# Branch rows, residual rows and output weights get buffers of their own, and key transpositions are queued ahead of the softmax

## The chip, the cores and the metric

One core of one Trainium2 chip runs the whole program. The metric is the device time of one execution in microseconds (us), as the median of several runs. Less is better.

## What is computed

One step of a decoder layer in fp32 for two groups of tokens with the same weights: a prompt of 512 tokens (with 16 learned meta tokens ahead of it) and 8 sample requests of 8 tokens each, which attend to 2048 cached tokens in pages. In the kernel both groups are 576 columns (512 prompt, 64 sample).

```python
h = rmsnorm(x)                                  # 1024 wide
q, k, v, log_f, ..., gate_f, gate_g = split(h @ w_in)
o_fox = softmax(q k^T * scale + forget bias) v  # prompt: causal; sample: 2048 cached + 8 new tokens
o_gla = gated linear attention(...)             # chunked, with a state
merged = sigmoid(gate_f) * (o_fox @ w_fox_out) + sigmoid(gate_g) * (o_gla @ w_gla_out)
x = x + merged @ w_o
x = x + hier_moe(rmsnorm(x))                    # 32 experts: y += gate_e * ((silu(h w_g) * (h w_u)) w_d)
y = rmsnorm(x)
```

## The kernel before

**Numbers in two halves.** A large product is computed as three: each fp32 operand is split by `split` (L119) into a rounded high half (ScalarE, L123) and a low half, the difference (VectorE or GpSimd, L125), and `mm3` (L133) multiplies high by high, high by low and low by high. So every tile of weights (`wh`, `wl` from `w`) and every input (`ofh`, `ofl`, `ogh`, `ogl`) needs one ScalarE and one VectorE or GpSimd instruction ahead of TensorE.

**Stages.** First come norm, projections and the prompt's attention. From about 215 us on, the sample requests are worked off in small steps (`sample_steps`, L1009) between steps of other work: linear attention at first, and all along `dense`, a stream of projections of 24 matmuls a step that fills TensorE. In this stage TensorE's order is the program's order; a scheduler orders the other engines from dependencies and priorities, and each engine then works its own queue strictly in order. At about 563 us the stream ends; `merge` (L1066), the output projection `out_proj` (L1114) with the routing, and the experts (`moe`) follow.

**A sample request.** Keys and values arrive as gathered pages of 128x2048, four key pages (K) and four value pages (V) a request, issued on GpSimd's queue (POOL, L892) into rings of three buffers each. A key page is transposed in place on VectorE (`turn`, L1016), one ahead of its use; then 32 small matmuls make scores (S, L925). Behind the fourth page stands the softmax (L938 to L961, VectorE and ScalarE in turns), then transpositions of its result on TensorE (`tp<-ident,SP`, L967), then the products with V (L987). The step of the fourth page in `sample_s` runs up to the end of the softmax, and only then does the loop call `turn` for the next request's page. `QB` (L901) is the copy of a request's queries on POOL.

**The merge.** The prompt's branch results lie in DRAM (`ofd`, `ogd`); the last request's 64 columns lie in SBUF (`ofS`), and L1610 writes them to `ofd` when the last request is done. `merge` then loads both branches whole (`oraw`, L1073), splits them, loads two gate rows (`gt`, L1084) and loops over 8 column blocks of the output with two branches each: load a weight, split it, 48 matmuls, gate it on VectorE (`mt`).

**The output projection.** For 4 blocks of 256 columns a pair of weight tiles (`woh`, `wol`) is made in a ring `wo` of 2; the residual `x2` is loaded (L1127, L1128) behind the first pair's weights on SyncE's queue (SP), and every group of 24 matmuls is added onto it (L1139).

**The experts** read three weights of 1 MiB each: gate and up in one tile `wgu` (ring of 4 `wxg` + 1 `wxh`), down in `wdn` (2 `wxd` + 3 `wxe`). The first tiles of each ring are loaded ahead, from the start of the merge; afterwards each pair of experts asks for the tiles of a later pair, which wait for a free buffer.

## Time and profile before

| what | us |
|---|---|
| median of 3 runs | 1028.68 (1026.78 to 1032.39) |
| the profiled execution: its own time | 1023.5 |
| its span (first to last instruction) | 1021.8 |
| its mean granted TensorE clock | 0.949 |
| TensorE (PE) busy | 904.5 (89%) |
| VectorE (DVE) / ScalarE (ACT) / GpSimd (POOL) busy | 496.8 / 288.4 / 227.4 |

TensorE is busy nearly all the time, so a change matters where it idles or runs at a lower clock. Times below are us from the start of the span; a clock of 1.00 is 2.4 GHz, 0.50 is 1.2 GHz. In a timeline row a bracket at the end is the idle time ahead of the instruction and what ended it.

### The profile page before, as it was taken

To read this page: it belongs to the slowest core of one execution; us is meant where nothing else is said; L and a number is where in the kernel's file an instruction comes from. 1 tells how busy PE (TensorE), PEld (TensorE's weight loads), DVE (VectorE), ACT (ScalarE), POOL (GpSimd) and SP (SyncE) were. 2 spreads that over 40 slices of the span, in tenths; PEclk is the share of its full clock that TensorE was granted. 3 is DMA by queue.
4 is the path that set the end of the run, shared out by engine and by line. 5 is a ranking of instruction groups with operands and counts; after the bars stand their busy time and mean duration, and the time that the engine had idled before them with its cause. 6 is when DMAs were issued, how large, how long until landed. Compare 5 with 4: busy or idle time off the path is not lost.

```text
span 1021.8 us, 18903 instructions
## 1 busy us (share of the span) xinstructions
PE 904.5 (89%) x7768; PEld 695.1 (68%) x7768; DVE 496.8 (49%) x1123; ACT 288.4 (28%) x640; POOL 227.4 (22%) x354
## 2 busy tenths in 40 slices
PE   3989989986989899897899598699699999999994
PEld 3878868775879799886898598699434443444342
DVE  5643454549565558564651367115424432443345
ACT  4223445323142223322321233005321121112113
POOL 5320101324254323342210145012400000000001
PEclk9999979988899899998999799799799999999998
DMA  7243222196378778789989757811789999999712
GB/s 202 72 121 96 77 58 60 50 345 203 117 240 294 259 253 266 236 303 333 339 283 331 262 175 194 280 62 63 256 358 404 417 389 377 379 415 384 315 42 94
DMA packets 124319, 240.23 MB, mean 235 GB/s; under 512 B 15516, under 2 KB 89132, under 8 KB 107844
## 3 DMA queue, kind: packets, MB, share of 16 engines
q1 hardware_dynamic: 107700, 161.05, 45.2%
q0 software_dynamic: 11664, 72.36, 19.4%
q10 hardware_dynamic: 4864, 5.57, 1.6%
q8 instruction: 62, 1.02, 0.4%
q14 instruction: 29, 0.24, 0.1%
HBM read 226.66 MB, written 15.96 MB: 237 GB/s over the span
## 4 chain that ended last, share of the span: by engine, by line
PE 72%; DVE 9%; DMA 7%; ACT 4%; issue 3%; POOL 3%; another core or an unknown queue 0%; SPq 0%; POOLq 0%; DVEq 0%; ACTq 0%
PE pj L138 26%; PE pj L1330 11%; PE ab L1330 7%; PE dn L1330 5%; PE pj L1136 5%; PE S L925 3%; PE tp L987 2%; DVE K L1016 2%; PE tp L1333 2%; DMA V<-in_cache_v_dram,idx 1%; DMA x<-in_x_prompt_dram 1%; PE G L523 1%; DMA w<-in_w_o_dram 1%; PE tp L736 1%; DMA oraw<-ofd 1%
## 5 line engine op out<-in xcount | busy, mean ns | idle before, releaser
L138 PE MATMUL pj<-hth,wh 128*128 128x288 f32 (+2 forms) x656 | 207.5, 316 | 1.8 <-DVE kt L381 1.8
L138 PE MATMUL pj<-htl,wh 128*128 128x288 f32 (+2 forms) x656 | 200.2, 305 | 0.0
L138 PE MATMUL pj<-hth,wl 128*128 128x288 f32 (+2 forms) x656 | 199.8, 305 | 0.0
L138 PEld LDWEIGHTS pj<-hth,wh 128*128 128x128 f32 (+1 forms) x656 | 127.1, 194 | 11.7 <-issue 7.3
L138 PEld LDWEIGHTS pj<-htl,wh 128*128 128x128 f32 (+1 forms) x656 | 127.1, 194 | 1.2 <-issue 0.8
L138 PEld LDWEIGHTS pj<-hth,wl 128*128 128x128 f32 (+1 forms) x656 | 126.4, 193 | 1.1
L1330 PE MATMUL pj<-wgu,xt 128*64 128x512 f32 x512 | 118.6, 604 | 0.6
L1330 PEld LDWEIGHTS pj<-wgu,xt 128*64 128x64 f32 x512 | 38.1, 138 | 61.4 <-issue 56.6
L125 DVE TENSOR_TENSOR wl<-w,wh 128x1024 fp32r<-128x1024 f32 (+1 forms) x41 | 51.7, 1261 | 52.9 <-ACT wh L123 48.7
L1016 DVE STREAM_TRANSPOSE K<-K 128x2048 f32<-128x2048 f32 x32 | 73.6, 2301 | 0.4 <-DMA K<-in_cache_k_dram,idx 0.3
L123 ACT ACTIVATE wh<-w 128x1024 fp32r<-128x1024 f32 (+2 forms) x57 | 52.6, 925 | 60.4 <-PE pj L138 54.8
L1330 PE MATMUL ab<-yh,S 128*128 128x512 f32 (+1 forms) x160 | 66.6, 416 | 1.0 <-DVE x L1402 0.9
L1330 PE MATMUL ab<-yl,S 128*128 128x512 f32 (+1 forms) x160 | 62.9, 393 | 0.0
L1402 DVE TENSOR_TENSOR x<-x,ab 128x512 f32<-128x512 f32 (+1 forms) x80 | 54.5, 684 | 17.3 <-PE ab L1330 17.3
L925 PE MATMUL S<-K,QB 128*32 128x128 f32 x1024 | 38.8, 298 | 27.2 <-DVE K L1016 23.5
L1362 DVE SCALAR_TENSOR_TENSOR th<-th,pj 128x256 f32<-128x256 f32 x16 | 6.7, 421 | 112.1 <-ACT th L1361 112.1
L1330 PE MATMUL dn<-wdn,heT 128*64 128x512 f32 x256 | 57.7, 593 | 0.7 <-ACT heT L1371 0.7
L1303 POOL DMA_INDIRECT xg<-h2d,ix x16 | 16.1, 1005 | 182.4 <-PE tp L1333 180.4
L925 PEld LDWEIGHTS S<-K,QB 128*32 128x32 f32 x1024 | 29.6, 119 | 31.3 <-issue 24.8
L892 POOL DMA_INDIRECT V<-in_cache_v_dram,idx x32 | 31.5, 986 | 62.1 <-PE tp L987 42.3
L1330 PEld LDWEIGHTS dn<-wdn,heT 128*64 128x64 f32 x256 | 18.4, 137 | 36.8 <-issue 35.9
L1330 PEld LDWEIGHTS ab<-yh,S 128*128 128x128 f32 (+1 forms) x160 | 28.3, 177 | 21.5 <-DVE x L1402 14.6
(426 smaller groups left out, 1605.3 us busy)
## 6 DMA issues: line engine op xcount, KB each, us to landing
wgu<-in_w_expert_gate_dram SPq DMA_DIRECT2D x32, 1024.0 KB
wgu<-in_w_expert_up_dram SPq DMA_DIRECT2D x32, 1024.0 KB
wdn<-in_w_expert_down_dram SPq DMA_DIRECT2D x32, 1024.0 KB
w<-in_w_in_dram SPq DMA_DIRECT2D x40, 512.0 KB
gtd<-sm ACTq DMA_DIRECT2D x32, 144.0 KB
gt<-gtd SPq DMA_DIRECT2D x8, 576.0 KB
R<-rdr SPq DMA_DIRECT2D x16, 256.0 KB
w<-in_w_o_dram SPq DMA_DIRECT2D x8, 512.0 KB
```

Of the source, the lines that this page charges most:

```text
L123: keep(nc.scalar.activation(hi, raw, AF.Copy))
L125: keep(e.tensor_tensor(lo, raw, hi.bitcast(F32), op=OP.subtract))
L138: nc.tensor.matmul(ps, lhsT=w[:, kt, :], rhs=r[:, kt, cs], start=(kt == 0 and j == 0), stop=(kt == nk - 1 and j == 2))
L892: nc.gpsimd.indirect_dma_start(t, None, view, bass.IndirectOffsetOnAxis(ap=self.idx[:, which, i:i + 1], axis=0)))
L925: nc.tensor.matmul(S[32 * h4:32 * h4 + 32, hf, x * 128:(x + 1) * 128], lhsT=QB[:, hb].rearrange("p a b -> p (a b)"), rhs=Kv[:, hb], start= ...
L987: nc.tensor.matmul(po[32 * c:32 * c + 32, 0:128], lhsT=PTv[:, c // 2, x, g, :], rhs=vt[:, o + c * 128:o + c * 128 + 128], start=(n == 0), ...
L1016: self.tc.keep_in_program_order(nc.vector.transpose(t, t))
L1136: nc.tensor.matmul(ps[:w, 0:256], lhsT=M[s][:, a, kt, ts], rhs=b[:, kt, :], start=(kt == 0 and j == 0), stop=(kt == 7 and j == 2))
L1303: self.nc.gpsimd.indirect_dma_start(xg, None, self.h2d[:, :], bass.IndirectOffsetOnAxis(ap=col, axis=0), bounds_check=NQ - 1, oob_is_err=F ...
L1330: self.tc.keep_in_program_order(self.nc.tensor.matmul(*a, **kw))
L1333: self.tc.keep_in_program_order(self.nc.tensor.transpose(*a))
L1402: self.tc.keep_in_program_order(nc.vector.tensor_tensor(x, x, ps[:w], op=OP.add))
```

## The change

1. `turn()` is called in `sample_s` right behind each page's matmuls, so for the fourth page ahead of the softmax code instead of behind it.
2. New `branch_inputs`: once the linear attention has released its buffers, the branches' rows are loaded in 4 + 4 pieces (only the prompt's 512 columns of the first branch) and split on ScalarE and GpSimd, while the last requests run. The last request's 64 columns are split straight from `ofS`; the way through DRAM is gone. One step of `dense` is taken ahead of the last loop.
3. The first two gate rows are loaded before the stream ends (`gate_rows`).
4. `x2` has a buffer of its own and is loaded before `merge`.
5. The output weights lie in tiles of the experts' shape in a ring `wxo`, which later serves the experts: `wgu` ring of 6 (4 + 2), `wdn` ring of 4 (2 + 2). The early `wgu` loads now wait for buffers that come free after `merge`.

```diff
-    def sample_s(self, r, sw, keys):
+    def sample_s(self, r, sw, keys, turn):
...
                                          rhs=Kv[:, hb], start=(b == 0), stop=(b == 1))
+            turn()
         nc.gpsimd.memset(PN, 0.0)
...
                 if what == "s":
                     n += 1
-                    turn()
                 yield
...
+    def branch_inputs(self, op):
+
+        nc, hl = self.nc, []
+        with self.pool("obr", 1) as rp:
+            for nm, src, n in (("f", self.ofd, 512), ("g", self.ogd, NQ)):
+                raw = rp.tile([128, 4, n], F32, name=f"raw{nm}")
                 h = op.tile([128, 4, NQ], F32R, name=f"o{nm}h")
                 l = op.tile([128, 4, NQ], F32R, name=f"o{nm}l")
-                self.split(raw, h, l)
+                for m in range(4):
+                    nc.sync.dma_start(raw[:, m], src[m, :, 0:n])
+                    self.split(raw[:, m], h[:, m, 0:n], l[:, m, 0:n], "pool")
                 hl.append((h, l))
+        return hl
...
-            if not n:
-                nc.sync.dma_start(self.x2[:, 0:4, :], A["x_prompt"][0].rearrange("(i p) d -> p i d", p=128))
-                nc.sync.dma_start(self.x2[0:64, 4, :], A["x_sample"].rearrange("r t d -> (r t) d"))
...
+        up(5, **late)
...
-            for e in (5, 6):
+            for e in (6, 7):
                 up(2 * ep + e, pin=True)
-            for e in (3, 4) if ep else ():
+            for e in (2, 3) if ep else ():
                 dn(2 * ep + e, pin=True)
...
+                op = self.open("ohl", 1)
+                hl = self.branch_inputs(op)
+
+                step(dense)
                 while step(S):
                     step(S)
                     step(dense)
-                nc.sync.dma_start(self.ofd[:, :, 512:576].rearrange("m p t -> p m t"), self.ofS)
+                for x, y in zip(hl[0], (nc.scalar, nc.vector)):
+                    x = x[:, :, 512:576]
+                    if y is nc.scalar:
+                        y.activation(x, self.ofS, AF.Copy)
+                    else:
+                        y.tensor_tensor(x, self.ofS, hl[0][0][:, :, 512:576].bitcast(F32), op=OP.subtract)
+                mt = self.open("mtm", 2)
+                gs = [self.gate_rows(mt, m) for m in range(2)]
...
+            wo = self.ring("wxo", 2, side="right")
+            self.x2 = xp.tile([128, 5, D], F32, name="x2")
+            nc.sync.dma_start(self.x2[:, 0:4, :], A["x_prompt"][0].rearrange("(i p) d -> p i d", p=128))
+            nc.sync.dma_start(self.x2[0:64, 4, :], A["x_sample"].rearrange("r t d -> (r t) d"))
+            M = self.merge(mt, hl, gs)
...
-                self.moe(mp, gp, [Ring(wxg.pools + wxh.pools), Ring(wxd.pools + wxe.pools)])
+                self.moe(mp, gp, [Ring(wxg.pools + wo.pools), Ring(wxd.pools + wxe.pools)])
```

VectorE's queue at the softmax of the first request, before: the end of this softmax, with the key transposition behind it (L958, L961 are the softmax's last instructions, `sc`, `ge`, `rsT`, `sx` belong to the linear attention).

```order
L882 STREAM_TRANSPOSE ogd<-ogc 128x32
L958 RECIPROCAL srl<-ogd 128x2
L961 TENSOR_SCALAR PN<-PN,srl 128x8 x2
L1016 STREAM_TRANSPOSE K<-K 128x2048
L495 TENSOR_TENSOR ge<-ge,qgT 128x144x2
```

And in the changed kernel, the start of the same softmax (L939 is its first instruction, the maximum of the scores).

```order
L529 COPY_PREDICATED sc<-lmask,G 128x32x16
L495 TENSOR_TENSOR ge<-ge,qgT 128x32x8
L1017 STREAM_TRANSPOSE K<-K 128x2048
L939 ISA R,smx<-S,R 128x512
L939 ISA smx 128x1
L939 ISA R,smx<-S,R 128x512
L939 ISA smx 128x1
L941 TENSOR_TENSOR sN<-tp,nb 128x16
```

The transposition that stood behind the softmax's last instruction now stands ahead of its first; it is so for most requests, and for two of them it stands between or behind the two maxima.

GpSimd's queue in the last third of the sample stage (the gathers around the query copy of the last request, `QB_1889`), before:

```order
L892 DMA K<-in_cache_k_dram,idx 128x2048
L892 DMA V<-in_cache_v_dram,idx 128x2048 x2
L901 COPY QB_1889<-QT 32x16x8 x4
L892 DMA K<-in_cache_k_dram,idx 128x2048 x2
L927 MEMSET PN 128x256
L892 DMA V<-in_cache_v_dram,idx 128x2048
```

And in the changed kernel, from the fifth low half on (ahead of it stand the query copy and four `ofl<-rawf,ofh 128x512`):

```order
L125 TENSOR_TENSOR ogl<-rawg,ogh 128x576
L892 DMA V<-in_cache_v_dram,idx 128x2048
L125 TENSOR_TENSOR ogl<-rawg,ogh 128x576 x3
L892 DMA K<-in_cache_k_dram,idx 128x2048
L892 DMA V<-in_cache_v_dram,idx 128x2048
L892 DMA K<-in_cache_k_dram,idx 128x2048 x2
```

The first K, V, V of the rows of before now stand behind the query copy and behind five to eight low halves.

SyncE's queue at the end of the stream, before:

```order
L1313 DMA wgu<-in_w_expert_gate_dram 128x2048 x3
L1610 DMA ofd<-ofS 128x4x64
L1313 DMA wgu<-in_w_expert_up_dram 128x2048
L1073 DMA oraw<-ofd 128x4x576
L1073 DMA oraw<-ogd 128x4x576
L130 DMA w_6542<-in_w_fox_out_dram 128x4x128
```

And in the changed kernel, from the merge's first weights on:

```order
L130 DMA w_6503<-in_w_fox_out_dram 128x4x128
L130 DMA w_6538<-in_w_gla_out_dram 128x4x128
L1317 DMA wdn<-in_w_expert_down_dram 128x2x1024
L130 DMA w_6580<-in_w_fox_out_dram 128x4x128
L1159 DMA gk<-in_norm_ffn_g_dram 128x8
L1317 DMA wdn<-in_w_expert_down_dram 128x2x1024
L1631 DMA x_6498<-in_x_prompt_dram 128x4x1024
```

The branch loads and gate rows have left this place (they stand some 15 rows earlier, ahead of the loads of the last projections), the residual has come to it, and the `wgu` loads stand behind the whole merge.

## Rows read from the trace of the kernel before

**Rows 1.** Busy time by stage: the stretch, its length, busy time (and instructions) of PE, PE weight loads, DVE, ACT, POOL, the granted clock, the share of the DMA engines, GB/s.

```profile
563.30:581.00 17.70, 6.54 (x26) 5.96 (x27) 5.93 (x4) 5.71 (x5) 2.52 (x2) 0.69 0.93 339
...
732.75:1000.00 267.25, 265.89 (x1217) 120.77 (x1217) 101.19 (x166) 51.39 (x129) 14.08 (x16) 0.99 0.85 343
```

**Rows 2.** The chain of work that ended last, 553 to 660 us: start, length, what.

```profile
554.32 4.15 DMA ofd<-ofS
558.53 8.89 DMA oraw<-ofd
...
572.19 7.74 DMA gt<-gtd
...
640.73 8.58 DMA x<-in_x_prompt_dram
```

**Rows 3.** Timeline of PE from the end of the stream of projections to the output projection: start, length, instruction, and in brackets the idle time ahead of it and its releaser.

```profile
569.62 0.85 PE L138 MATMUL pj<-ofh,wh 128*128 128x256 f32 x2 [6.32 <-ACT ofh L123]
...
572.21 0.58 PE L138 MATMUL pj<-ofl,wh 128*128 128x256 f32 x1 [1.74 <-DVE ofl L125]
...
580.62 0.55 PE L138 MATMUL pj<-ogh,wh 128*128 128x256 f32 x1 [3.10 <-DVE mt L1093]
...
628.51 0.36 PE L138 MATMUL pj<-ogh,wh 128*128 128x256 f32 x1 [1.70 <-DVE mt L1093]
...
632.48 0.42 PE L138 MATMUL pj<-ogh,wh 128*128 128x320 f32 x1 [2.31 <-DVE mt L1093]
...
634.36 2.08 PE L1136 MATMUL pj<-woh,htl 128*128 128x256 f32 x16
...
649.88 3.78 PE L1136 MATMUL pj<-woh,hth 128*128 128x256 f32 x16 [9.60 <-DVE x L1139]
```

**Rows 4.** Two stretches by the clock, columns as in rows 1.

```profile
566.80:577.00 10.20, 5.64 (x22) 5.29 (x23) 5.12 (x2) 4.25 (x2) 0.00 (x0) 0.50 1.06 391
...
645.30:655.50 10.20, 5.62 (x26) 5.62 (x27) 0.85 (x3) 0.00 (x0) 0.00 (x0) 0.50 1.05 382
```

**Rows 5.** Merge alone (first) and output projection alone (second) at full clock: length, PE busy and matmuls, weight loads, clock, DMA share, GB/s.

```profile
584.00:616.00 32.00, 32.00 (x244) 32.00 (x243) 1.00 0.55 166
...
656.00:692.00 36.00, 35.88 (x297) 35.53 (x296) 1.00 0.25 91
```

**Rows 6.** Timeline of PE in the sample stage: the first scores of the second, third, seventh and eighth request, and the transpositions of a softmax result (SP).

```profile
257.31 1.94 PE L925 MATMUL S<-K,QB 128*32 128x128 f32 x32 [10.24 <-DVE K L1016]
...
265.51 0.66 PE L967 MATMUL tp<-ident,SP 128*128 128x128 f32 x4
...
306.36 1.94 PE L925 MATMUL S<-K,QB 128*32 128x128 f32 x32 [3.66 <-DVE gss L613]
...
312.65 0.60 PE L967 MATMUL tp<-ident,SP 128*128 128x128 f32 x4
...
478.30 1.94 PE L925 MATMUL S<-K,QB 128*32 128x128 f32 x32 [6.89 <-DVE K L1016]
...
509.07 1.08 PE L925 MATMUL S<-K,QB 128*32 128x128 f32 x32 [1.24 <-DVE K L1016]
```

**Rows 7.** Timeline of DVE at the end of the first softmax.

```profile
254.85 2.31 DVE L1016 STREAM_TRANSPOSE K<-K 128x2048 f32<-128x2048 f32 x1
```

**Rows 8.** Timeline of ACT: the last instructions of the softmax of the first and of the sixth request, which make SP.

```profile
254.93 1.32 ACT L960 ACTIVATE SP<-SP,srl 128x512 f32<-128x512 f32 x2
...
475.50 1.33 ACT L960 ACTIVATE SP<-SP,srl 128x512 f32<-128x512 f32 x2 [3.74 <-DVE srl L958]
```

**Rows 9.** Timeline of POOL around the query copy of the last request.

```profile
460.93 0.94 POOL L892 DMA_INDIRECT V<-in_cache_v_dram,idx  x1 [0.87 <-PE tp L987]
465.30 0.94 POOL L892 DMA_INDIRECT K<-in_cache_k_dram,idx  x1 [3.43 <-PE S L925]
...
469.94 0.28 POOL L901 COPY QB<-QT 32x128 f32<-32x128 f32 x1
480.98 0.94 POOL L901 COPY QB<-QT 32x128 f32<-32x128 f32 x3 [10.76 <-issue]
```

**Rows 10.** Tile K, 425 to 545 us: from a gather's issue to its landing.

```profile
DMA to landing us min/median/max: 6.4/6.7/7.0
```

**Rows 11.** Splits by form, 200 to 720 us: line, engine, operation, tile, shape, count, then busy time and mean ns of one, then idle time ahead of them.

```profile
L125 DVE TENSOR_TENSOR wl<-w,wh 128x1024 fp32r<-128x1024 f32 x26 | 34.1, 1313 | 21.3 <-ACT wh L123 17.1 <-issue 4.2
...
L125 POOL TENSOR_TENSOR wl<-w,wh 128x512 fp32r<-128x512 f32 x16 | 22.6, 1415 | 61.8 <-ACT wh L123 61.8
...
L123 ACT ACTIVATE wh<-w 128x512 fp32r<-128x512 f32 x16 | 10.1, 631 | 20.0 <-PE pj L138 20.0
```

**Rows 12.** Timeline of DVE, one split of 128x1024.

```profile
234.77 3.71 DVE L125 TENSOR_TENSOR wl<-w,wh 128x1024 fp32r<-128x1024 f32 x1
```

**Rows 13.** Two stretches of the last requests, columns as in rows 1.

```profile
450.00:475.00 25.00, 20.65 (x348) 18.17 (x346) 14.88 (x33) 6.41 (x16) 9.05 (x14) 0.99 0.89 312
475.00:500.00 25.00, 20.20 (x321) 18.76 (x322) 12.14 (x16) 4.69 (x7) 6.77 (x10) 0.87 0.92 294
```

**Rows 14.** Waits of SyncE's queue, 560 to 1000 us: who waited for what, us in total, times, the longest.

```profile
SPq L1313 <- PE pj L1330: 164.4, 14, 17.4
```

**Rows 15.** The end of the experts, columns as in rows 1.

```profile
950.00:975.00 25.00, 24.93 (x120) 10.55 (x117) 7.17 (x12) 6.40 (x16) 0.00 (x0) 1.00 0.71 274
975.00:1000.00 25.00, 24.21 (x106) 10.54 (x105) 10.93 (x18) 3.92 (x8) 0.00 (x0) 1.00 0.03 10
```

More of the change, by code (lines that the diff above doesn't have):

```diff
@@ L1079, in merge @@
+    def merge(self, tp, hl, gs):
+        nc, A = self.nc, self.A
         M = {0: self.big.tile([128, 2, 8, 256], F32R, name="htl"), 256: self.big.tile([128, 2, 8, 320], F32R, name="hth")}
         late = []
-        with self.pool("mtm", 2, side="right") as tp:
-            def gate(m):
-                g = tp.tile([128, 2, NQ], F32, name="gt")
-                nc.sync.dma_start(g, self.gtd[2 * m:2 * m + 2].rearrange("b p t -> p b t"))
-                return g
-            gs = [gate(0), gate(1)]
-            for m in range(8):
-                t = [None, None]
-                gm = gs.pop(0)
-                if m and m < 7:
-                    gs.append(gate(m + 1))
-                def evac(ps, cs):
-                    nc.vector.scalar_tensor_tensor(t[b][:, cs], gm[:, b, cs], 1.0, ps, op0=OP.add, op1=OP.mult)
-                    while late:
-                        late.pop()()
-                    if b:
-                        x, h, l = t[0][:, cs], M[cs.start][:, 0, m], M[cs.start][:, 1, m]
-                        nc.vector.tensor_tensor(x, x, t[1][:, cs], op=OP.add)
-                        nc.scalar.activation(h, x, AF.Copy, scale=0.5)
-                        late.append(lambda: nc.vector.scalar_tensor_tensor(l, x, 0.5, h.bitcast(F32), op0=OP.mult, op1=OP.subtract))
-                for b, wn in ((0, "w_fox_out"), (1, "w_gla_out")):
-                    raw = self.wraw(A[wn][0, :, m * 128:(m + 1) * 128], 4, 128)
-                    if not m:
-                        self.mload = self.lastw
-                    wh = self.wp.tile([128, 4, 128], F32R, name="wh")
-                    wl = self.wp.tile([128, 4, 128], F32R, name="wl")
-                    self.split(raw, wh, wl, "pool")
-                    t[b] = tp.tile([128, NQ], F32, name=f"mt{b}")
-                    for _ in self.halves(wh, wl, 4, hl[b][0], hl[b][1], NQ, evac, 256):
-                        pass
-            late.pop()()
@@ new lines, in merge, with evac @@
+        for m in range(8):
+            t = [None, None]
+            gm = gs.pop(0)
+            if m and m < 7:
+                gs.append(self.gate_rows(tp, m + 1))
+            def evac(ps, cs):
+                nc.vector.scalar_tensor_tensor(t[b][:, cs], gm[:, b, cs], 1.0, ps, op0=OP.add, op1=OP.mult)
+                while late:
+                    late.pop()()
+                if b:
+                    x, h, l = t[0][:, cs], M[cs.start][:, 0, m], M[cs.start][:, 1, m]
+                    nc.vector.tensor_tensor(x, x, t[1][:, cs], op=OP.add)
+                    nc.scalar.activation(h, x, AF.Copy, scale=0.5)
+                    late.append(lambda: nc.vector.scalar_tensor_tensor(l, x, 0.5, h.bitcast(F32), op0=OP.mult, op1=OP.subtract))
+            for b, wn in ((0, "w_fox_out"), (1, "w_gla_out")):
+                raw = self.wraw(A[wn][0, :, m * 128:(m + 1) * 128], 4, 128)
+                if not m:
+                    self.mload = self.lastw
+                wh = self.wp.tile([128, 4, 128], F32R, name="wh")
+                wl = self.wp.tile([128, 4, 128], F32R, name="wl")
+                self.split(raw, wh, wl, "pool")
+                t[b] = tp.tile([128, NQ], F32, name=f"mt{b}")
+                for _ in self.halves(wh, wl, 4, hl[b][0], hl[b][1], NQ, evac, 256):
+                    pass
@@ L1112, in merge, with out_proj @@
+        late.pop()()
         return M
-    def out_proj(self, M, xp, wp):
+    def out_proj(self, M, wp):
         nc, A = self.nc, self.A
-        self.x2 = xp.tile([128, 5, D], F32, name="x2")
         for n in range(4):
             with self.tc.high_priority(offset=400):
-                wt = wp.next()
-                wh = wt.tile([128, 8, 256], F32R, name="woh")
-                wl = wt.tile([128, 8, 256], F32R, name="wol")
+                wt = wp.next().tile([128, 2, 8, 256], F32R, name="wgu")
+                wh, wl = wt[:, 0], wt[:, 1]
@@ L1427, in moe @@
                 up(e, ahead=300)
-            for e in range(5):
+            for e in range(4):
                 dn(e, ahead=300)
@@ L1618, in build @@
             spp.release()
-            with self.pool("ohl", 1, side="right") as op:
-                M = self.merge(op)
-            self.wp.release()
             xp = top.enter_context(self.pool("x2p", 1, side="right"))
@@ L1624, in build @@
             wxd = self.ring("wxd", 2, side="right")
+            wo = self.ring("wxo", 2, side="right")
[3 more added lines that the diff above has]
+            M = self.merge(mt, hl, gs)
+            for p in (mt, op, smq, self.cp2, self.wp):
+                p.release()
             wxg = self.ring("wxg", 4, side="right")
[L1626 removed]
             rp = self.open("rt", 1, side="right")
             self.route(rp)
[L1629 removed]
+            self.out_proj(M, wo)
             self.sp8.release()
```

25 lines of the change are left out of this document (7 added, 18 removed).

## The prediction

> **What bounds the kernel now.** I read the busy time by stage first. TensorE is the bound in the experts (265.89 of 267.25 us busy [rows 1]), and there is nothing to win. Around the merge it is not: between 563.30 and 581.00 it works 6.54 of 17.70 us, at a mean clock of 0.69. The chain of waits says why [rows 2]: the last request's columns go to DRAM (4.15 us), come back with the whole branch (8.89), and the gate rows follow (7.74); later the residual's load (8.58) stands in the chain as well. Third, the timeline of TensorE, where the reader is to see each of these as idle time in brackets [rows 3]: 6.32 ahead of the merge's first matmul, so the stream of projections ends at 569.62 - 6.32 = 563.30; then 1.74 for the second half, 3.10 for the gating that lacks its gate rows, and 9.60 in the output projection, where the sum onto the residual can't run. Fourth, the clock: after each of these waits it is granted at 0.50 for 10.20 us [rows 4]. Last the sample stage [rows 6]: four scores wait for a key page, 10.24, 3.66, 6.89 and 1.24 us. At the first of them VectorE shows the cause: the transposition of 2.31 us that the scores wait for begins at 254.85 [rows 7], when the softmax of the request before is over.
>
> **The change, step by step.**
>
> *Merge.* From 563.30 to the output projection's first matmul at 634.36 are 71.1 us [rows 3]. The merge is 8 blocks x 2 branches x 24 = 384 matmuls; 244 of them take 32.00 us at full clock [rows 5], so all take 50.4. Of the 20.7 us over, the waits of 1.70 and 2.31 at its end stand behind the last blocks' gating, which isn't touched, and stay; 16.7 go: 11.2 of idle time (6.32 + 1.74 + 3.10) and some 5.5 of half clock. What could be late next: the branch rows must be split by then. They are loaded some 90 us earlier, behind the linear attention's last rows. The 64 new columns cost one ScalarE and one VectorE instruction, far shorter than the 8.89 of the load, under the last steps of the stream. The low half of the second weight needs a buffer that the stream's last step frees; 0.63 on ScalarE and 1.42 on GpSimd [rows 11] lie under the first 24 matmuls (24 x 0.131 = 3.1). The residual and two down weights (some 4.4 MB) now load beside the first blocks; one weight could come a few us late. I take 16.7 off, with 11.2 (clock and a late weight eat the rest) and 20.7 as ends.
>
> *Residual.* It is loaded a whole merge ahead, so the 9.60 go. After them 26 matmuls took 5.62 us at half clock [rows 4]; at 35.88 / 297 = 0.121 [rows 5] they take 3.1, so 2.5 more: 12.1 off. Ends: 9.6 and 12.1. The next thing needed there, the second pair of output weights, is asked for at the same place in the queues as before, and has the 15 us of the first five groups as cover.
>
> *Key transposition.* It leaves the end of the softmax for its start, which frees the scores but makes the softmax 2.3 us longer; the next consumer of the softmax on TensorE, its transposition SP, stands one projection step behind the scores. First case: without the wait the second request's scores start at 257.31 - 10.24 = 247.1. From scores to SP were 8.2 us [rows 6], part of it at half clock (scores of 1.94 against 1.08 in the row at 509.07); at full clock I estimate 5.7. So TensorE reaches SP at 252.8. The result was ready at 254.93 + 1.32 [rows 8], now 2.3 later at 258.6: a wait of 5.8 takes the place of 10.24, 4.4 off. Third request: 3.66 go, and the 3.1 us of the projection step cover the 2.3: 3.7 off. Eighth: 1.24 moves to SP, nothing. Seventh: the 6.89 move to SP as well, since the result is ready at 475.50 + 1.33 = 476.8 plus 2.3, where TensorE would stand from 473.4 (471.4 and 2 us of scores). Here the new work adds to it.
>
> *Branch rows in the last requests.* Eight loads (some 2.25 MB) and the gate rows move into a stretch whose DMA share is already 0.89 to 0.92 [rows 13]. Eight high halves of some 0.63 each stand on ScalarE, most of them ahead of that softmax's exponentials; the deadline they pass there is worth 2.3 (they are 5 us in all, and VectorE is 2.3 later anyway). So SP waits from 473.4 to 481.4, 8.0 for 6.9: 1.1 lost. Eight low halves of 1.4 to 1.6 us, some 12 us, stand on GpSimd ahead of gathers. In the rows of before the key page of 465.30 was gathered ahead of the query copy; now it stands behind the copy, which waits for gathers in flight (10.76 us idle there) [rows 9], and behind all eight. If the copy waits about as long for the value page gathered at 460.93, it runs at some 472 and the halves end at about 485; 6.7 to land [rows 10] and 2.3 to transpose make 494, where the scores used it at 491.7: 2.3 lost. Together 3.4 lost, where the pieces land in time; ends 0 and 14 (all low halves and 2 us of ScalarE on the path).
>
> The sample stage thus gives 4.4 + 3.7 - 3.4 = 4.7. Its upper end is all four waits (22.0) and three recoveries of the clock at 2.5: 29. Its lower end is 8.1 - 14 = -6.
>
> The Trainium skill (Trainium Architecture — The Big Picture, What this means for kernel authors) says that VectorE and GpSimd contend for a shared pair of SBUF ports, under an exclusive lock. One row here fits it: a split of 128x1024 on VectorE that takes 1.31 in the mean [rows 11] took 3.71 [rows 12]. By that rule the 12 us of low halves would also be up to 12 us of delay for VectorE; it would bring the sample stage to its lower end, the first rival below.
>
> *Experts.* Residual, output weights and rings move bytes, not work. The early gate and up tiles (8 MB) are asked for after the merge rather than from 544 on; at the 343 GB/s of the experts' stage [rows 1] they take some 25 us, and TensorE needs them some 85 us after the merge (732.75 - 634.36, less 12.1). Rings of 6 and 4 hold 16 MB, those of 5 and 5 15. SyncE waits for TensorE there (164.4 us, 14 times [rows 14]) and the DMA share falls to 0.03 while TensorE still works 24.21 of 25 us [rows 15]: loads are ahead. Nothing.
>
> The Trainium skill (DMA: Bandwidth & Descriptors, Issuing engines are not separate DMA queues) says that transfers of all issuers share the same 16 engines. The 0.89 to 0.92 agree; by it the 2.25 MB cost up to 7 us at the 312 GB/s of that stretch, which lies inside the range.
>
> **Sum.** 16.7 + 12.1 + 4.7 = 33.5. The profiled execution's 1023.5 becomes 990.0; the median of the runs stands 5.2 above it, so I say 1028.7 - 33.5 = 995.
>
> **Rivals.**
> 1. The last requests give back what the first ones gain and more: low halves and gathers collide, the sample stage loses 6. For it: the full DMA stretch and POOL's strict order; against: K and V have rings of three. 1028.7 - 28.8 + 6 = 1006.
> 2. All key waits go, the softmax isn't waited for: 28.8 + 29 = 57.8, 971. For it: other requests run with no wait at all; against: the results' times in rows 8.
> 3. Slower: GpSimd is held until the branch rows land and the last requests' gathers stand behind it. Two branches at 8.89 are 17.8, the halves 12, the clock three times 2.5: 37 us of idle TensorE, which is where it cancels 28.8 + 8.1; from there on it is slower, at 45 us some 1037. For it: SyncE's queue, where the rows stand ahead of projection weights; against: pieces land one by one and the first is split at once.
> 4. Experts wait for down weights, with four buffers in place of five. It decides at 33.5 / 16 = 2.1 us a pair, at 3 us some 1043. Against: rows 14 and 15.
> 5. The residual or the branch rows get their buffers late and their waits stay: half of the 28.8 isn't won, 1010.
>
> **Chances.** Forecast (980 to 1003) 0.55; first rival 0.22; second 0.12; third 0.04; fourth 0.03; fifth 0.04. About 0.5% (5 us) is what a measurement here can tell from no change. Faster 0.92, same 0.04, slower 0.04. The range of 8 in 10 goes from the second rival's edge, 973, to the first and fifth with the merge's lower end, 1028.7 - 11.2 - 9.6 + 5 = 1013.
>
> **What would show it.** Right: no idle time over 1 us between the stream and the merge, none ahead of the third group of the output projection, the clock at 1.00 in both; scores of the second request without a wait and SP with one of 5 to 6. Wrong: idle TensorE ahead of scores or V products of the last two requests with a gather as releaser (rivals 1, 3); idle time ahead of `dn` in the experts (4); the first merge matmul waiting for a low half of a branch (5).

## The result

The changed kernel took 1004.62 us, beside 1027.86 for the kernel before on the same chip: a ratio of 0.9761 (95% interval 0.9729 to 0.9793). Run again on another chip it took 995.82 beside 1024.38, ratio 0.9735 (0.9693 to 0.9776). One of the first four executions ran at a mean granted clock of 0.65 and took 1275.11 us; the ratio leaves it out. So the change wins 21 to 31 us; the forecast was 33.5, with 973 to 1013 as its range. The first time lies above the 980 to 1003 of the forecast itself, the second within it.

The profile after is of an execution of 1004.81 us, with a span of 1003.1. I cut each profiled execution at five places of TensorE's timeline: the first scores of the first and of the fifth request, the end of the stream of projections, the first matmul of the output projection, and the first work of the experts. These are the lengths between them in us, for every kernel run (the labels are those of the experiments below):

```
                          start  req. 1-4  req. 5-8, stream  merge  out_proj  experts    span
before                    219.9     180.6             162.8   71.1      98.4    289.0  1021.8
after                     223.7     176.9             171.0   55.3      86.3    290.0  1003.1
after_again               219.1     174.2             167.5   55.4      86.3    288.3   990.8
e1_turn_old               217.7     183.8             168.8   55.7      87.2    289.2  1002.4
e2_turn_only              221.3     175.6             161.2   71.7      97.1    288.3  1015.2
e3_inputs_end             217.4     174.0             158.2   67.3      87.7    288.6   993.0
e4_x2_late                219.4     173.3             169.2   57.2      86.3    289.7   995.1
e5_low_dve                220.6     176.7             168.4   55.6      88.2    289.0   998.5
e6_split_late             221.1     176.3             168.3   55.8      88.5    288.6   998.7
e8_rows_early_split_late  219.0     174.1             163.0   57.3      87.1    289.2   989.7
e9_qb_act                 222.7     166.8             166.3   56.7      86.9    289.8   989.2
e10_two_loads             218.9     171.1             163.6   55.2      86.7    288.8   984.2
e11_x2_held               219.2     175.3             171.5   55.6      98.8    289.0  1009.4
e12_before_qb_act         216.7     178.3             157.9   72.3      98.2    288.9  1012.3
```

The first column, in which all kernels do the same work (in `e9`, `e10` and `e12` with the first query copies on another engine), differs by 7 us between single executions, and the columns of the sample stage by some 4 between kernels with the same code there; the last three agree to 1 or 2. The two profiles of the changed kernel differ by 12 us this way: 4.5 lie in the first column, 6.1 in the sample stage, 1.6 in the experts. Where the code is the same I therefore take means over several kernels.

**Merge.** The stretch of [rows 1] and [rows 3], in TensorE's timeline after. The merge's first matmul (second row) follows on the last of the projections (first row) without idle time; waits for the gating are all that is left, at its end:

```profile
571.16 0.30 PE L138 MATMUL pj<-hth,wl 128*128 128x288 f32 x1
571.30 0.28 PE L138 MATMUL pj<-ofh,wh 128*128 128x256 f32 x1
...
621.37 0.35 PE L138 MATMUL pj<-ogh,wh 128*128 128x256 f32 x1 [1.84 <-DVE mt L1096]
624.94 0.41 PE L138 MATMUL pj<-ogh,wh 128*128 128x320 f32 x1 [1.92 <-DVE mt L1096]
626.80 3.39 PE L1134 MATMUL pj<-wgu,htl 128*128 128x256 f32 x27
...
632.55 8.72 PE L1134 MATMUL pj<-wgu,hth 128*128 128x256 f32 x72
```

The last two rows are of the output projection: where [rows 3] have 9.60 us ahead of its third group, nothing waits.

Busy time of the merge and of the output projection's first 36 us, with the columns of [rows 1]. The clock is 1.00 in both, in place of the half clock of [rows 4]:

```profile
571.46:626.97 55.51, 51.66 (x387) 51.02 (x386) 32.47 (x62) 19.29 (x35) 24.08 (x20) 1.00 0.68 202
...
627.00:663.00 36.00, 36.00 (x303) 35.88 (x302) 12.00 (x22) 5.35 (x6) 8.07 (x4) 1.00 0.83 286
```

**First requests.** TensorE around the second request's scores, in answer to [rows 6]. The wait of 10.24 ahead of the scores is gone; two others have come, one for `ge`, an operand of the linear attention, and one for the softmax result SP:

```profile
249.92 1.08 PE L925 MATMUL S<-K,QB 128*32 128x128 f32 x32
260.06 1.98 PE L523 MATMUL G<-ge 64*128 64x64 f32 x16 [5.67 <-POOL ge L494]
266.42 1.11 PE L968 MATMUL tp<-ident,SP 128*128 128x128 f32 x4 [4.04 <-ACT SP L961]
```

GpSimd at that time: `ge` stands behind the query copies, which wait for a key gather.

```profile
256.80 1.12 POOL L901 COPY QB<-QT 32x128 f32<-32x128 f32 x3 [8.02 <-DMA K<-in_cache_k_dram,idx]
...
259.21 1.67 POOL L494 TENSOR_TENSOR ge<-ge,kgT 128x288 f32<-128x288 f32 x2
```

Before, such a `ge` stood ahead of the copies:

```profile
245.99 1.09 POOL L494 TENSOR_TENSOR ge<-ge,kgT 128x288 f32<-128x288 f32 x1 [0.43 <-ACT ge L493]
...
253.33 1.38 POOL L901 COPY QB<-QT 32x128 f32<-32x128 f32 x3 [6.02 <-DMA K<-in_cache_k_dram,idx]
```

And VectorE: the sum of the softmax (M, L956) stands behind `sc`, which waits for TensorE's product of that same `ge`. So in this execution both new waits hang on `ge`; `e9_qb_act` below shows that the second stays without that.

```profile
262.43 0.69 DVE L529 COPY_PREDICATED sc<-lmask,G 128x512 f32<-128x512 uint8 x1 [5.33 <-PE G L528]
263.04 0.15 DVE L956 TENSOR_TENSOR M<-sl 128x2 f32<-128x2 f32 x1
```

The third request's scores, at 306.29, don't wait either. Their 3.66 us in [rows 6] are put down to `gss`, an operand of the linear attention, and not to a key page. On VectorE `gss` stood directly behind a transposition, so it was late with it:

```profile
304.00 2.30 DVE L1016 STREAM_TRANSPOSE K<-K 128x2048 f32<-128x2048 f32 x1
306.23 0.12 DVE L613 TENSOR_SCALAR gss<-gss 128x2 f32<-128x2 f32 x1
```

**Seventh request.** The fifth request's first scores start at 400.51, and at 400.54 before, so the two traces can be laid on each other here. TensorE, around the seventh's first scores, which waited 6.89 us in [rows 6]:

```profile
479.38 0.33 PE L1001 MATMUL tp<-ident,SO 128*128 128x128 f32 x1 [4.17 <-ACT SO L998]
479.64 1.23 PE L925 MATMUL S<-K,QB 128*32 128x128 f32 x32
488.94 1.12 PE L968 MATMUL tp<-ident,SP 128*128 128x128 f32 x4 [8.08 <-ACT SP L961]
```

ScalarE ahead of that: it stands 7.04 us at the first branch row, put down to the row's landing, with the copy SO and the exponentials (L953) behind it. In `e1_turn_old`, `e4_x2_late`, `e5_low_dve` and `e11_x2_held`, which split the rows there as well, the profile names the same load (4.56 to 7.07 us); in the second profile of the changed kernel it names a query copy (5.84).

```profile
474.22 2.51 ACT L123 ACTIVATE ofh<-rawf 128x512 fp32r<-128x512 f32 x4 [7.04 <-DMA rawf<-ofd]
...
479.06 0.26 ACT L998 ACTIVATE SO<-tp 128x128 f32<-128x128 f32 x1
...
479.80 0.71 ACT L953 ACTIVATE SP<-R,sb 128x512 f32<-128x512 f32 x1
...
488.17 1.34 ACT L961 ACTIVATE SP<-SP,srl 128x512 f32<-128x512 f32 x2 [5.43 <-DVE srl L959]
```

VectorE had the factor `sb` for the first exponential ready at 472.83, 7 us ahead of its use. Then its sum of 128x2 numbers, 0.16 us in the median of the eight requests, takes 4.67:

```profile
472.67 0.16 DVE L948 TENSOR_TENSOR sb<-aq,ogd 128x2 f32<-128x2 f32 x1
481.90 4.67 DVE L956 TENSOR_TENSOR M<-sl 128x2 f32<-128x2 f32 x1 [9.08 <-ACT PN L955]
```

It ends with the last of three low halves on GpSimd (the rows that answer to [rows 9]):

```profile
474.99 4.95 POOL L125 TENSOR_TENSOR ofl<-rawf,ofh 128x512 fp32r<-128x512 f32 x4 [1.67 <-ACT ofh L123]
...
482.45 4.10 POOL L125 TENSOR_TENSOR ogl<-rawg,ogh 128x576 fp32r<-128x576 f32 x3
486.71 0.96 POOL L892 DMA_INDIRECT K<-in_cache_k_dram,idx  x1 [0.16 <-DVE M L956]
```

### The profile page after: what moved, and what is told of

Its sections match the earlier page's. It is cut to its first block, busy times and chain, and to the rows that moved or that the text cites. A ratio compares the mean times of both kernels' runs of the same rounds, so it can differ in the third digit from the quotient of the medians.

```text
span 1003.1 us, 18937 instructions
## 1 busy us (share of the span) xinstructions
PE 902.7 (90%) x7768; PEld 692.8 (69%) x7768; DVE 496.3 (49%) x1122; ACT 288.1 (29%) x647; POOL 236.8 (24%) x364
## 5 line engine op out<-in xcount | busy, mean ns | idle before, releaser
L138 PEld LDWEIGHTS pj<-hth,wh 128*128 128x128 f32 (+1 forms) x656 | 128.3, 196 | 11.6 <-issue 7.1
L892 POOL DMA_INDIRECT K<-in_cache_k_dram,idx x32 | 32.4, 1013 | 40.0 <-PE S L925 19.9
L1386 DVE SCALAR_TENSOR_TENSOR yl<-dn,gate,yh 128x512 fp32r<-128x512 f32 x32 | 24.0, 751 | 35.0 <-ACT yh L1385 35.0
```

The source lines that it names most:

```text
L138: nc.tensor.matmul(ps, lhsT=w[:, kt, :], rhs=r[:, kt, cs], start=(kt == 0 and j == 0), stop=(kt == nk - 1 and j == 2))
L892: nc.gpsimd.indirect_dma_start(t, None, view, bass.IndirectOffsetOnAxis(ap=self.idx[:, which, i:i + 1], axis=0)))
L1386: nc.vector.scalar_tensor_tensor(yl[:, nh], dn, gate, yh[:, nh].bitcast(F32), op0=OP.mult, op1=OP.subtract)
```

## The experiments

Ratios are against the kernel before on the same chip; unless it is said otherwise the edit is made to the changed kernel.

### The first requests: the transposition alone, and everything else without it

`e1_turn_old` puts `turn` back behind the softmax; `e2_turn_only` is the kernel before with that one edit.

```diff
-            turn()
         nc.gpsimd.memset(PN, 0.0)
...
                 if what == "s":
                     n += 1
+                    turn()
                 yield
```

> The changed kernel with the key transposition back behind the softmax. Stretches by the trace: first scores of request 1 to first scores of request 5 took 180.6 us before and 176.9 changed; from there to the end of the stream 162.8 before and 171.0 changed. Theory A (the branch pieces in the last requests cost the late loss, the transposition gave the early gain): early stretch back to about 180.6, late stretch stays at 170 to 172, in all some 4 us slower than the changed kernel, about 1008. Theory B (the longer softmax costs the late loss, the branch pieces are free): late stretch back to about 163, in all 4 us faster, about 1000.

> The kernel before with the moved key transposition alone. Theory A: early stretch about 177, late stretch about 163, merge unchanged at 71.1: some 4 us faster than before, about 1024. Theory B: early 177, late about 171, in all 4 us slower than before, about 1032.

Measured: without the moved transposition 1003.38 us, ratio 0.9787 (0.9756 to 0.9818); the moved transposition alone 1012.57, ratio 0.9882 (0.9851 to 0.9912), 12 us faster than before. Both theories had expected it within some 4 us of the kernel before. The profiled execution, the slowest of its four, shows 6.6 of the 12, all in the sample stage. In the changed kernel the times alone don't tell whether the moved transposition helps: the ratio of `e1_turn_old` lies 3 to 5 us above those of the changed kernel, with intervals that overlap. Its first four requests take 183.8 us, where the kernels with the moved transposition and the same copies take 173.3 to 176.9. TensorE's timeline of the first shows the old wait again, and that of the second no wait ahead of the second request's scores, and the seventh's wait moved to SP:

```profile
255.16 1.93 PE L925 MATMUL S<-K,QB 128*32 128x128 f32 x32 [10.34 <-DVE K L1016]
```

```profile
247.49 1.08 PE L925 MATMUL S<-K,QB 128*32 128x128 f32 x32
257.86 1.97 PE L523 MATMUL G<-ge 64*128 64x64 f32 x16 [5.90 <-POOL ge L494]
...
469.61 1.08 PE L925 MATMUL S<-K,QB 128*32 128x128 f32 x32
474.89 1.12 PE L968 MATMUL tp<-ident,SP 128*128 128x128 f32 x4 [4.20 <-ACT SP L961]
```

So the longer softmax doesn't cost what the last requests lose: with the moved transposition alone they take 161.2 us up to the end of the stream (162.8 before), without it, but with all the rest, 168.8. The loss belongs to another part of the change; the next runs look for it in the branch rows.

### The branch rows: at the old place, and in two other ways

`e3_inputs_end` keeps every other part and loads the branches whole at the end, through DRAM as before. `e6_split_late` loads the rows behind the projection weights issued last and splits them, with the low halves on VectorE, behind the last request's softmax. `e5_low_dve` only takes the low halves from GpSimd to VectorE. `e8_rows_early_split_late` loads as the changed kernel does and splits as `e6_split_late` does.

```diff
# e3_inputs_end (each branch in one load, split in one go: left out)
...
-                hl = self.branch_inputs(op)
...
+                st = nc.sync.dma_start(self.ofd[:, :, 512:576].rearrange("m p t -> p m t"), self.ofS).ins
+                with tc.issue_after(st):
+                    hl = self.branch_inputs(op)
# e5_low_dve
-                    self.split(raw[:, m], h[:, m, 0:n], l[:, m, 0:n], "pool")
+                    self.split(raw[:, m], h[:, m, 0:n], l[:, m, 0:n])
# e8_rows_early_split_late
-                    self.split(raw[:, m], h[:, m, 0:n], l[:, m, 0:n], "pool")
+                    todo.append((raw[:, m], h[:, m, 0:n], l[:, m, 0:n]))
...
+            yield hl
+            for t in todo:
+                self.split(*t, pin=True)
...
# e6_split_late: as e8, and
...
+                    if self.stage == 1 and bi is None:
+                        with tc.issue_after(self.lastw):
+                            bi = self.branch_inputs(op)
+                            hl = next(bi)
```

> The changed kernel with the branch inputs as before: last columns through DRAM, both branches loaded whole behind the last request, low halves on VectorE, gate rows behind them. Residual and rings stay changed. Both theories: the way from the end of the stream to the output projection back from 55.3 to about 71. Theory A: late stretch back to about 163, so 8 us slower than the changed kernel, about 1012. Theory B: late stretch stays at 171, 16 us slower, about 1020.

Measured: 997.64 us, ratio 0.9759 (0.9713 to 0.9805), where both theories had it 8 us or more slower than the changed kernel. The merge takes 67.3 us, 12 more than after, and the last requests 158.2, 11.6 less than in the kernels that have the change's branch rows (171.0, 167.5, 169.2 and 171.5 in after, after_again, e4 and e11, mean 169.8). **On balance the branch rows, which were to win most of the 16.7, win nothing**: the two kernels can't be told apart by their times. The gate rows go back to the end together with the branch rows here, and no run moves them alone.

> The changed kernel with the branch rows loaded behind the last projection weights and split (low halves on VectorE) behind the last request's softmax and its copies. Theory A: late stretch about 163, merge stays at 55 to 57, in all 7 us faster than the changed kernel, about 997. Theory B: late stretch stays at 171, about 1004.

Measured: 997.40 us, ratio 0.9731 (0.9701 to 0.9761), the same as the changed kernel. The time is the one expected, the stretch is not (168.3 us, 163 expected). The seventh request is undisturbed, but the eighth loses more: TensorE waits 10.52 us for PT, the transposed softmax result that the products with V read, with ScalarE at a projection weight.

```profile
522.31 0.66 PE L988 MATMUL tp<-VN,PT 128*32 128x128 f32 x8 [10.52 <-DVE PT L975]
```

```profile
507.64 0.41 ACT L1060 ACTIVATE sm<-pj 128x288 f32<-128x288 f32 x1 [5.70 <-DMA gtd<-sm]
517.04 0.33 ACTq L1061 DMA_DIRECT2D gtd<-sm  x1
517.41 1.06 ACT L123 ACTIVATE wh<-w 128x1024 fp32r<-128x1024 f32 x1 [9.36 <-DMA w<-in_w_in_dram]
```

```profile
504.53 2.42 SPq L130 DMA_DIRECT2D w<-in_w_in_dram  x1
507.05 8.00 SPq L1076 DMA_DIRECT2D rawf<-ofd  x4
```

The weight of 512 KB was issued at 504.53 and split only at 517.41. Two things stand ahead of that split. One is the load: the busy time of that stretch, with the columns of [rows 1], has the DMA engines full, and GpSimd's queue, the gathers, took 72.2% of the engines' time from 504.5 to 511.

```profile
505.00:520.00 15.00, 6.79 (x76) 6.19 (x74) 2.85 (x4) 1.76 (x3) 0.31 (x1) 0.85 1.06 329
```

So GpSimd's gathers and SyncE's loads worked on the same engines at that time, as the Trainium skill (DMA: Bandwidth & Descriptors, Issuing engines are not separate DMA queues) leads one to expect. The branch rows themselves can have delayed the weight only in part: the first of the eight loads was issued at 507.05, the other seven from 513.76 on.

The other is a store of gate rows (`gtd`) on ScalarE itself. Its data was ready at 508.05, and it was issued at 517.04, directly ahead of the split. Which of the two held ScalarE isn't shown.

> The changed kernel once more, on the chip of the other runs of this call. Stretches: first scores of request 1 to request 5 some 177 us, from there to the first scores of request 8 some 117 (108.5 before), from there to the end of the stream 54, to the output projection 55. The time ahead of the first scores differs from run to run by some 6 us with the clock.

> The changed kernel with the eight low halves of the branches on VectorE in place of GpSimd; the scheduler still puts them, and the high halves, into the sixth request's softmax. If GpSimd's halves slow VectorE (one instruction of 0.16 us took 4.67 beside three of them), that instruction is back at some 0.2 us and the stretch of 117 becomes 112; what is left over 105 is ScalarE, held until the rows land. If they don't matter, it stays at 117.

Measured: the changed kernel again as told above; VectorE's low halves 1002.11 us, ratio 0.9784 (0.9736 to 0.9831), no gain. From the first scores of the fifth to those of the eighth request it takes 114.8 us, where 112 was expected if the stretch mattered and 117 if not. The stretched sum is gone, but ScalarE's wait is not, and TensorE still waits 4.08 for SO and 6.30 for SP:

```profile
483.48 0.12 DVE L956 TENSOR_TENSOR M<-sl 128x2 f32<-128x2 f32 x1
```

```profile
471.94 0.63 ACT L123 ACTIVATE ofh<-rawf 128x512 fp32r<-128x512 f32 x1 [7.07 <-DMA rawf<-ofd]
```

In all five profiles with low halves on GpSimd one small VectorE instruction takes 4.27 to 4.77 us beside them; in `e1_turn_old` and `e11_x2_held` it is not the sum but a copy some instructions later:

```profile
474.75 4.77 DVE L880 COPY ogc<-ogb 128x32 f32<-128x32 f32 x1
```

So the stretch is real and comes with the low halves on GpSimd, but isn't, by itself, what the last requests pay for.

> The changed kernel with the branch rows loaded where it loads them, but split (low halves on VectorE) only behind the last request's softmax and its copies. Theory A (ScalarE's and GpSimd's queues cost the late loss, not the bytes): 177, 105, 54 and 56 us in the four stretches, so 11 us faster than the changed kernel, ratio to before some 0.965. If the bytes cost it: 117 stays, ratio 0.976.

Measured: 991.20 us, ratio 0.9689 (0.9652 to 0.9725), and 163.0 us for the last requests. Loads at the same place, splits behind the last softmax (and the low halves on VectorE, which won nothing in `e5_low_dve`): 6.8 us of the 169.8 come back. By the times, against the changed kernel on the same chip, it is 4.7, with intervals that overlap. What is left is a smaller wait of SP, with ScalarE held ahead of a store of gate rows that the profile puts down to the branch rows' landing:

```profile
471.61 0.65 PE L968 MATMUL tp<-ident,SP 128*128 128x128 f32 x4 [2.47 <-ACT SP L961]
```

```profile
465.12 0.33 ACTq L1061 DMA_DIRECT2D gtd<-sm  x1
465.49 0.28 ACT L998 ACTIVATE SO<-tp 128x128 f32<-128x128 f32 x1 [2.28 <-DMA rawf<-ofd]
```

### The residual: the place in the code, and the buffer

`e4_x2_late` moves the loads of `x2` back to the place in the code where they stood. `e11_x2_held` does the same and also keeps the buffer busy: two copies of one element from the merge's last low half into `x2`, which the loads must wait for.

```diff
             if not n:
+                last = M[256][:, 1, 7, 0:1].bitcast(F32)
+                nc.vector.tensor_copy(self.x2[:, 0, 0:1], last)
+                nc.vector.tensor_copy(self.x2[0:64, 4, 0:1], last[0:64])
                 nc.sync.dma_start(self.x2[:, 0:4, :], A["x_prompt"][0].rearrange("(i p) d -> p i d", p=128))
```

> The changed kernel with the residual loaded where the kernel before loads it, behind the first pair of output weights on SyncE's queue, into the buffer of its own. The way from the output projection's first matmul to the experts' first took 98.4 us before and 86.3 changed. If the early load is worth its whole 12.1 us (9.6 of wait and 2.5 of half clock), it is back at 97 to 98 and the kernel is 12 us slower than the changed one, ratio to before some 0.986. If something else took the wait (the queue is shorter there now, the early expert weights come later), it stays under 92.

Measured: 997.03 us, ratio 0.9714 (0.9654 to 0.9773): not slower, against what I expected. SyncE's queue shows why. The buffer is free, and the load is issued early from the later place in the code too:

```profile
557.86 0.45 SPq L1128 DMA_DIRECT2D x<-in_x_prompt_dram  x1
```

> The changed kernel, the residual's buffer kept busy until the merge's last low half is written: two one-element copies from that low half into x2 make its loads wait, and they stand on SyncE's queue where they stood before, behind the second pair of output weights. Theory A (what won the 12 us is that the buffer is free early, not the place in the code): the wait ahead of the third group of the output projection comes back with some 9 us of idle TensorE and the half clock behind it, output projection to experts 97 to 99 us against 86.3, some 12 us slower than the changed kernel (about 1007, ratio 0.983 to 0.988). Theory B (the shorter stage came from the later gate and up loads, which leave the output weights alone): no wait, 86 to 88 us, the same time as the changed kernel.

Measured: 1010.12 us, ratio 0.9848 (0.9832 to 0.9864), 9 to 12 us slower than the changed kernel by the ratios, all of it in the output projection's stretch (98.8 for 86.3). The load is issued as late as before, 6.8 us behind the first matmul of the output projection (6.4 before). In both timelines it stands behind seven of the eight loads of output weights, and not behind the first pair alone. The wait is back:

```profile
628.42 0.38 SPq L1131 DMA_DIRECT2D x<-in_x_prompt_dram  x1
```

```profile
624.71 4.21 PE L1140 MATMUL pj<-wgu,htl 128*128 128x256 f32 x33 [1.13 <-DVE htl L1103]
637.80 11.05 PE L1140 MATMUL pj<-wgu,hth 128*128 128x256 f32 x72 [8.88 <-DVE x L1143]
```

So it is the buffer that wins the 12 us, and neither the load's place in the code nor the later loads of gate and up weights.

### The query copies

The copies that held `ge` read nothing that is gathered. `e9_qb_act` is `e8_rows_early_split_late` with the copies on ScalarE, `e12_before_qb_act` the kernel before with that edit alone, and `e10_two_loads` is `e9_qb_act` with one load for each branch in place of four.

```diff
-            nc.gpsimd.tensor_copy(self.QB[r % 2][s, :, g, :], self.QT[s, rh, :, 8 * rq:8 * rq + 8])
+            nc.scalar.activation(self.QB[r % 2][s, :, g, :], self.QT[s, rh, :, 8 * rq:8 * rq + 8], AF.Copy)
# e10_two_loads
-                    nc.sync.dma_start(raw[:, m], src[m, :, 0:n])
+                nc.sync.dma_start(raw, src[:, :, 0:n].rearrange("m p t -> p m t"))
```

> As the run before, with the query copies on ScalarE in place of GpSimd. If the linear attention's factor that GpSimd makes behind the query copy (which waits there for gathers in flight) is what the second request waits for (5.7 us, then 4.0 for the softmax result), the first stretch falls from 177 to some 169 to 172, and the ratio to some 0.96. If the wait has another cause it stays at 177.

> The kernel before, with the query copies on ScalarE and nothing else. Theory A (the copies cost only what stands behind them on GpSimd, the linear attention's ge, and this shows only once the second request no longer waits 10 us for its key page): the first four requests stay at 178 to 181 us, total within 3 us of the kernel before (ratio 0.997 to 1.0). Theory B (copies that wait for a gather cost wherever they stand): first four requests shorter by some 7 us, ratio 0.993.

Measured: on top of the late splits 986.66 us, ratio 0.9622 (0.9591 to 0.9654); in the kernel before 1016.54, ratio 0.9916 (0.9900 to 0.9933). It is worth some 7 us in the one (0.9622 for 0.9689, intervals that just overlap) and 8.6 in the other. My theory that it pays only where the moved transposition has uncovered it, with at most 3 us in the kernel before, falls. Nor does the profile of `e12_before_qb_act` put the gain where the rival had it: requests 1 to 4 become 2.3 us shorter and the rest of the sample stage 4.9, with the waits for key pages of [rows 6] still there (10.32 and 7.21 us). Which of the later requests win by it stays open.

In `e9_qb_act` the second request's wait for `ge` falls to 2.75 us (4.84 in `e8_rows_early_split_late`) and is put down to VectorE. `sc` ahead of the sum (at 257.38) waits only 0.43, and yet TensorE waits 4.53 for SP. So SP's wait is there without the copies too.

```profile
255.99 1.11 PE L523 MATMUL G<-ge 64*128 64x64 f32 x16 [2.75 <-DVE ge L495]
261.86 1.12 PE L968 MATMUL tp<-ident,SP 128*128 128x128 f32 x4 [4.53 <-ACT SP L961]
```

> As the run e9_qb_act, with each branch's rows loaded in one transfer in place of four. There the sixth request's softmax stood still although nothing of the branches was split then: a store of gate values stood ahead of it on ScalarE's queue, issued 5.2 and 7.4 us after its data was ready. If that store waits for one of the eight row loads (they take up the completion counters that it needs), two loads free it: the stretch from request 5 to request 8 falls from 109 to some 103 to 105, ratio to before 0.956. If the bytes hold ScalarE, it stays at 109.

Measured: 987.47 us, ratio 0.9643 (0.9584 to 0.9701), not to be told from `e9_qb_act`. From the first scores of the fifth to those of the eighth request it takes 107.2 us (109.3 there), where 103 to 105 was expected. At one place it does what it was to do: in `e9_qb_act` the store of gate rows was held and SP came 9.57 us late, and with two loads SP waits 0.79. But then a later key page is 4.53 us late. ScalarE and TensorE in `e9_qb_act`, and TensorE in `e10_two_loads`:

```profile
470.14 0.33 ACTq L1061 DMA_DIRECT2D gtd<-sm  x1
470.51 1.33 ACT L961 ACTIVATE SP<-SP,srl 128x512 f32<-128x512 f32 x2 [7.78 <-DMA rawg<-ogd]
```

```profile
471.29 1.12 PE L968 MATMUL tp<-ident,SP 128*128 128x128 f32 x4 [9.57 <-ACT SP L961]
```

```profile
461.62 0.65 PE L968 MATMUL tp<-ident,SP 128*128 128x128 f32 x4 [0.79 <-ACT SP L961]
...
481.48 1.93 PE L925 MATMUL S<-K,QB 128*32 128x128 f32 x32 [4.53 <-DVE K L1017]
```

TensorE waits at another place, with the same 2.25 MB to be loaded; that these cause the later wait isn't shown. These two are the fastest kernels run, some 10 us faster than the changed kernel.

## Why the prediction was right, and where it was not

**Merge, 16.7: right.** The stretch went from 71.1 to 55.3 us, 15.7 less. The three waits went, the clock held, and the waits that were said to stay, 1.70 and 2.31 in [rows 3], stayed as 1.84 and 1.92.

**Residual, 12.1: right.** 98.4 to 86.3. `e11_x2_held` gives it back: 8.88 us of idle time, and 12.5 in the whole stretch.

**Experts, nothing: right.** 289.0, and 290.0 and 288.3 in the two profiles. SyncE's queue waits there as in [rows 14], 143.9 us over 13 waits.

**Sample stage, 4.7 gained: wrong, by the term on the branch rows.** From the first scores to the end of the stream it takes 343.4 us before and 344.7 in the mean of the four kernels named above (347.8, 341.7, 342.5, 346.8): 1.3 lost, or nothing. Of the 6.0 missed, 3.6 are the branch rows' and 2.4 the first four requests'. By its parts:

- First four requests: 8.1 forecast (4.4 + 3.7), 5.7 in the mean of the same four (174.9 for 180.6). The scores start without a wait at 249.92 and SP waits 4.04, near the 5.8 forecast; `sc` stands ahead of it there, but `e9_qb_act` has 4.53 without that, which fits the reason that the forecast gave, the longer softmax. What the forecast lacked is the 5.67 ahead of G: the `ge` that stood ahead of a waiting copy on GpSimd now stands behind it. I had read the copy's wait only in the last request [rows 9], and asked only who waits for gathers there. The third request's 3.66 went as told, though the prediction took it for a wait for a key page and the row names `gss`.
- Transposition in the seventh request: alone it leaves a wait of 4.20 (by the working, 476.8 plus 2.3 less 473.4, it would be 5.7). Right.
- Branch rows: the forecast was 3.4 lost, transposition included; measured were 7.0 (169.8 for 162.8). SP was to be ready at 481.4 and came at 488.94, and another 4.17 stand ahead of SO. That SP's own wait, 8.08, agrees with the 8.0 of the working is chance: it begins 7.5 us later than told. The failed step is "the deadline they pass there is worth 2.3", and with it the condition "where the pieces land in time". It priced the eight high halves at the 0.63 that each takes on ScalarE, and not what the first of them waits for. The split of a row that had not landed held all that stood behind it on ScalarE: the first row was issued at 462.17, and its split began only at 474.22. With the splits behind the last softmax (`e8_rows_early_split_late`) 6.8 us came back. The third rival had this mechanism, "held until the branch rows land", on GpSimd; it happened on ScalarE.
- The gather of a key page behind the low halves, 2.3 late: it was late as told (the copies ran at 472.37 and the halves ended at 486.55, where the working had 472 and 485; the gather was issued at 486.71, and gathers landed in 5.9 to 9.4 us where [rows 10] have 6.4 to 7.0). TensorE didn't wait for it, as it was later still.

The port rule of the Trainium skill that the prediction weighed (Trainium Architecture — The Big Picture, What this means for kernel authors) agrees with one row of the trace: 4.67 us for a sum that takes 0.16, beside three low halves on GpSimd, and 4.27 in the second profile. It isn't the 12 us that the rule's strictest reading gave, and `e5_low_dve` shows that taking it away wins nothing while ScalarE is held.

The total came out near because the two large terms were right: by the stages 26.5 us were won of the 33.5, all of them in the merge and the output projection. That the sample stage came out near nothing is gain and loss of like size, and by `e3_inputs_end` the branch rows lose there what they win in the merge. The first rival (1006, the last requests give back) is nearer to the first result, 1004.62, than the 995 of the forecast is: its mechanism was half right, with a loss of 1 rather than 6.

## What to carry to other kernels

Work that is moved early into a full stage must be priced on an in-order engine by what its first instruction waits for, not by how long it runs: load early, but put the splitting behind the last instruction that has a deadline. When a load is late, ask first for the buffer that it needs: with a buffer of its own the residual was early from both places in the code that were tried, and with that buffer held it was late again from the old one. And when one stall goes, look through the queue in which it was hidden for the next instruction that waits, here copies that needed nothing of what they waited for.

## What the runs showed of the hardware

- A VectorE sum of 0.16 us took 4.67 and 4.27 us beside three GpSimd instructions of 1.4 each, and 0.12 to 0.16 with those away; in `e1_turn_old` and `e11_x2_held` it was a copy of 0.18 us that took 4.77.
- Copies on GpSimd that read no gathered page waited 8.02 us, put down to a key gather issued on the same engine; the same copies on ScalarE (`e9_qb_act`, `e12_before_qb_act`) waited for no gather.
- ScalarE stood 7.78 us at a store that it issues, where the profile names the landing of a load on SyncE's queue that it doesn't read; with two loads in place of eight the softmax behind it came in time. What ties them together isn't shown by any row.
- 512 KB of weights were split 12.9 us after their issue (`e6_split_late`), with the DMA engines at a share of 1.06; what of that the load took, and what a store held on ScalarE ahead of the split, isn't shown.
